# The first quarter of a projection's depth taken in two halves, its modulation loaded by halves, and the first squares summed on TensorE

## The chip, the cores and the metric

The kernel runs on one core of a Trainium2 chip. The metric is the device time of one execution in microseconds; the time before is the median of three executions. Engines are named as in the profile: PE (TensorE) multiplies, DVE (VectorE), ACT (ScalarE) and POOL (GpSimd) work on elements, SP (SyncE) issues the transfers.

## The reference

One step of a two-layer transformer for 128 context tokens and 128 latent tokens. All that matters here is the first sub-layer of layer 0:

```
mod = silu(cond) @ w_ada[l] + b_ada[l]
sh1, sc1, gt1, sh2, sc2, gt2 = jnp.split(mod[:, None, :], 6, axis=-1)
h = rmsnorm(x, g_norm_mix[l]) * (1 + sc1) + sh1
proj = h @ w_in
```

`x` has 2048 features. `mod` is a product of two condition rows (context and latent) with a 2048 x 12288 matrix, and `proj` has 23 blocks of 128 columns. Everything is fp32. After it come the two attentions, the output projection, a convolutional FFN and a second layer of the same size; the change leaves these alone.

## The kernel before, in words

The features lie on the partitions: the residual stream `x` is 16 chunks of 128 features by 256 tokens. A weight product is made of two fp32r parts: a raw tile of weights is split into `wh` (ACT, L212) and `wl = raw - wh` (DVE, L213), and each block of 128 x 128 weights takes three PE products, `wh*hx_high`, `wh*hx_low` and `wl*hx_high` (L305, L306, L309 in `gemm` and `first_three`'s L291 to L293). A raw tile is 1 MB, 16 blocks; three buffers `raw` hold such tiles, four buffers `wh` and four `wl` hold half a tile each, three PSUM banks `acc` take the sums.

The first projection (`mixer_ab`, L732 to L753) goes over its depth in four quarters q of four chunks each. In each quarter the four chunks of `x` are modulated into `hx` (`modulate`, L476 to L509: DVE multiplies by the spread norm, DVE and ACT apply scale and shift, ACT casts the high part, DVE or POOL subtracts the low part), then 23 column blocks c are multiplied: 12 PE products each. ACT copies the sum of q=0 into `pr` or `qb` (L745); DVE adds those of q=1 to 3 to it (L747).

The modulation comes in **units** (l, j, q): 512 columns of part j (0 is the shift, 1 the scale) of layer l, 4 MB in four tiles of 1 MB. Unit order is the list `ROWS`: (0,1,0), (0,0,0), (0,1,1), (0,0,1) and so on, so units 0 and 1 serve quarter q=0, units 2 and 3 serve q=1, units 4 and 5 serve q=2. A tile is loaded into one of two buffers `araw` (L421) and multiplied by the condition in four PE instructions into the bank `ada` (L401, `sum_rows`); it is freed by this product. After the fourth tile, ACT copies the bank (L342), PE transposes it (L349), DVE reduces it and adds the bias (L358, L360), and for j=1 makes the scale (L367). `pump` calls `row_step` a number of times for each column block (`RATE["in"]` rows; a quarter of a tile a call), and `ensure` finishes the units that a quarter needs. In the start phase (`ada["both"]`) every second tile takes a `raw` buffer instead.

The norm of the stream (L1029 to L1034) squares the 16 chunks on ACT (L165, L168), adds them up on POOL (L172), sums over the partitions with four PE products (L192, L193); then `rstd` adds eps on DVE (L177) and takes the power on POOL (L179), `diagonal` scales the identity on DVE (L199) and `spread` multiplies it by ones on PE (L207).

The order on each engine is not the order of the text: a scheduler places the instructions of the program by its own estimate of times, within what the buffers allow, except those wrapped in `tc.keep_in_program_order`. Each engine, and SP's list of transfers, then keeps the built order: an instruction that waits holds up all behind it on its engine. The order of the built programs of both kernels is known before a run.

Of the kernel before, what the change touches and what calls it, by code (L numbers as in the profile page):

```python
# [17 lines left out]
P = 128  # L18
D = 2048
KD = D // P  # L20
T = 128
# [62 lines left out]
def step_kernel(ctx: ExitStack, tc: tile.TileContext, A: dict):  # L84
# [52 lines left out]
    def load_cw(l):  # L137
        ada["cw"] = T_(keep, [P, 4, 2 * NFF], "convw")
        sp.dma_start(out=ada["cw"], in_=A["wconv"][:, l])

# [32 lines left out]

    def rstd(ps, n):

        v = T_(small, [P, 2], "rv")
        dve.tensor_scalar(out=v[:, :n], in0=ps, scalar1=EPS, scalar2=None, op0=ALU.add)  # L177
# [10 lines left out]
    def stat_rstd(st, width, bank=bank):  # L188
        ps = bank()
        for g in range(2):  # L190
            t = slice(g * T, (g + 1) * T)
            pe.matmul(ps[:, g:g + 1], st["acc"][:, t], inv(width), start=True, stop=False)  # L192
            pe.matmul(ps[:, g:g + 1], st["last"][:, t], inv(width), start=False, stop=True)  # L193
        return rstd(ps[:, 0:2], 2)

# [117 lines left out]

    ada = {"i": 0, "t": 0, "due": 0.0, "pew": 1.0, "both": True}
    feat = {"i": 0, "t": 0, "due": 0.0}
    stage = ["ab"]
    pinned = [False]
    done = set()
    later = []

    def vector(name, l, j, q):
# [84 lines left out]
    def row_step(until=len(ROWS)):  # L406
# [9 lines left out]
        if g == 0:  # L416
            if ada["both"] and t % 2:
                ada["raw"] = T_(wpool, [P, 4, 512], "raw")
            else:
                ada["raw"] = T_(wpool, [P, 4, 512], "araw", bufs=2)  # L420
            sp.dma_start(out=ada["raw"], in_=A["w_ada"][l, j, q, t])  # L421
# [200 lines left out]
    def mixer_ab(hx, rb0, st):  # L622
        l = 0
        with tc.tile_pool(name="ab", bufs=1) as ab:
            with tc.tile_pool(name="abp", bufs=1) as pj:
# [7 lines left out]
                def caches():  # L633
                    sp.dma_start(out=ckc, in_=A["cache_ckv"])
                    split(kv_in[:, :, 0, T:2 * T], kv_in[:, :, 1, T:2 * T], ckc)
                    sp.dma_start(out=kr[:, T:2 * T], in_=A["cache_krope"])
                    sp.dma_start(out=kg[:, :, T:2 * T], in_=A["cache_gqa_k"])
                    sp.dma_start(out=vg[:, 1], in_=A["cache_gqa_v"])

# [49 lines left out]
                def keys(c):  # L689
# [7 lines left out]
                    r = rstd(pst[:, 0:2], 2)  # L697
                    yield
# [32 lines left out]

                W = Weights(A["w_in_ab"], 4, 4, cycle=23)  # L732
                for q in range(4):
                    ensure(0, 1, [q])
                    ensure(0, 0, [q])
                    ada["both"] = False
# [4 lines left out]
                    for c in range(23):  # L741
                        ps = gemm(W.chunk(), lambda k: hx[:, 4 * q + k, :NT], lambda k: hx[:, 4 * q + k, NT:2 * NT])
                        to = pr[:, c] if c < 15 else qb[:, c - 15]
                        if q == 0:
                            act.copy(to, ps)  # L745
                        else:
                            dve.tensor_tensor(out=to, in0=to, in1=ps, op=ALU.add)  # L747
                        if q == 3:
                            finish(c)
                        if q < 3:  # L750
                            pump(RATE["in"], until=2 * (q + 2))
                        else:
                            pump(RATE["in3"])  # L753

            with tc.tile_pool(name="abh", bufs=1) as hp:
# [10 lines left out]
                def gqa_query(h):  # L766
# [8 lines left out]
                    r = rstd(pst[:, 0:2], 2)  # L775
                    pool.tensor_scalar(out=rsb[:, h], in0=r[:, 0:2], scalar1=HEAD_SCALE,
# [322 lines left out]
def _layout(i):  # L1099
# [29 lines left out]

    a["w_ada"] = i["w_ada"].reshape(NL, 4, 4, P, 6, 4, 512).transpose(0, 4, 5, 1, 3, 2, 6).copy()  # L1130
    for l, j, q in FEATS:
        w = i["w_ada"][l][:, j * D + 512 * q:j * D + 512 * q + 512]
        a["w_ada"][l, j, q] = w.T.reshape(4, P, 4, 512)
# [4 lines left out]
    w = np.concatenate([w, np.zeros((D, P), np.float32)], 1)  # L1138
    a["w_in_ab"] = np.concatenate([_blocks(w[512 * q:512 * q + 512], range(24), 4) for q in range(4)])
    w = i["w_mla_q_up"][0].reshape(768, 8, 192)  # L1140
# [47 lines left out]
```

## Time and profile before

| | |
|---|---|
| median of three executions | 2388.5 us (2387.7 to 2389.89) |
| the profiled execution | 2393.79 us, its span 2391.9 us |
| PE busy | 2329.2 us, 97% of the span |
| first projection product | 40.30 us after the span's start |
| first product of q=1, of q=2, of q=3 | 85.89, 135.66, 179.04 us |

In the rows of the profile, a timeline row gives the start, the time, the engine, the line, the operation with what it writes and reads, and in brackets how long the engine had been idle and what ended this. Several like instructions in a row are merged (x4). The tile product of L401 is four instructions, counted as x8. A row of stretches gives for each engine its busy time and count, then the clock that TensorE was granted, the busy share of the transfer engines and GB/s. Lines with `L401` are the modulation products, `L305`, `L306` and `L309` the projection products.

### The profile page before, as it was taken

The page shows a single profiled execution, that of the slowest core. Times are in us where ns is not written, and L with a number is a line of the kernel's source. Part 1 is how long each engine was busy: PE and PEld are TensorE (multiplying, and loading weights), DVE is VectorE, ACT ScalarE, POOL GpSimd, SP SyncE. Part 2 cuts the span into 40 slices and gives each one's busy share as a digit, 9 for nine tenths or more (in the row PEclk, how much of TensorE's full clock was granted, in tenths as well). Part 3 has the DMA queues.
Part 4 walks back from the last instruction along what each step waited for, and adds up shares of the span by engine and source line. Part 5 has one row for each costly group of instructions (what it writes and reads, how often), then busy time and mean ns, then how long its engine had stood idle before and what let it go on. Part 6 is the DMA issues. An engine that isn't in the chain of part 4 may idle for free. (4 is left out here: it accounts for less than half of the span.)

```text
span 2391.9 us, 47275 instructions
## 1 busy us (share of the span) xinstructions
PE 2329.2 (97%) x19664; PEld 2189.5 (92%) x19664; DVE 1764.9 (74%) x2691; ACT 1165.7 (49%) x1815; POOL 180.2 (8%) x219
## 2 busy tenths in 40 slices
PE   6999999999999999999999999999999999999997
PEld 3778868789999999999989999997999999999997
DVE  2467534469999999999979777877899855666654
ACT  4335544365554345554465444445655534555542
POOL 2002101110000000001220000023000000000011
PEclk9999999999999999999999999999999999999998
DMA  9886678877777777777766787686667655555553
GB/s 382 310 338 239 235 265 306 311 274 256 263 262 282 289 276 263 264 264 264 303 229 237 279 296 293 257 301 260 249 250 261 214 194 194 194 194 194 194 194 120
DMA packets 92549, 612.92 MB, mean 256 GB/s; under 512 B 9968, under 2 KB 17840, under 8 KB 20400
## 3 DMA queue, kind: packets, MB, share of 16 engines
q1 hardware_dynamic: 92336, 609.91, 69.6%
q8 instruction: 154, 2.52, 0.4%
q14 instruction: 59, 0.48, 0.1%
HBM read 605.12 MB, written 4.75 MB: 255 GB/s over the span
## 5 line engine op out<-in xcount | busy, mean ns | idle before, releaser
L212 ACT CAST wh<-raw 128x1024 fp32r<-128x1024 f32 (+1 forms) x788 | 795.5, 1015 | 984.0 <-PE acc L306 823.6
L213 DVE TENSOR_TENSOR wl<-raw,wh 128x1024 fp32r<-128x1024 f32 (+1 forms) x788 | 921.6, 1183 | 390.7 <-ACT wh L212 384.7
L305 PE MATMUL acc<-hx,wh 128*128 128x256 f32 x4064 | 1132.9, 279 | 8.6 <-ACT hx L504 5.6
L309 PE MATMUL acc<-hx,wl 128*128 128x256 f32 x4064 | 1131.0, 279 | 0.0
L306 PE MATMUL acc<-hx,wh 128*128 128x256 f32 x4064 | 1130.2, 278 | 0.0
L305 PEld LDWEIGHTS acc<-hx,wh 128*128 128x128 f32 x4064 | 765.9, 189 | 34.8 <-issue 12.1
L306 PEld LDWEIGHTS acc<-hx,wh 128*128 128x128 f32 x4064 | 766.5, 189 | 13.8 <-issue 12.9
L309 PEld LDWEIGHTS acc<-hx,wl 128*128 128x128 f32 x4064 | 766.2, 189 | 12.2 <-issue 10.4
L306 PE MATMUL acc<-g,wh 128*128 128x256 f32 x1408 | 388.3, 276 | 0.0
L309 PE MATMUL acc<-g,wl 128*128 128x256 f32 x1408 | 388.0, 276 | 0.0
L305 PE MATMUL acc<-g,wh 128*128 128x256 f32 x1408 | 387.8, 276 | 0.0
L386 DVE CUSTOM_DVE_ANT_0 junk<-araw,condb 128x2048 f32<-128x2048 f32 x120 | 275.0, 2291 | 0.0
L306 PEld LDWEIGHTS acc<-g,wh 128*128 128x128 f32 x1408 | 264.3, 188 | 0.0
L309 PEld LDWEIGHTS acc<-g,wl 128*128 128x128 f32 x1408 | 264.2, 188 | 0.0
L305 PEld LDWEIGHTS acc<-g,wh 128*128 128x128 f32 x1408 | 264.1, 188 | 0.0
L172 POOL TENSOR_TENSOR sqacc<-sqacc,sq 128x256 f32<-128x256 f32 x76 | 93.0, 1223 | 1534.1 <-issue 1223.1
L401 PE MATMUL ada<-araw,condw 128*32 128x512 f32 x768 | 106.6, 628 | 19.3 <-DMA araw<-w_ada 18.5
L430 DVE SCALAR_TENSOR_TENSOR aacc<-araw,condw,aacc 128x512 f32<-128x512 f32 x150 | 111.8, 773 | 0.2
L553 DVE SCALAR_TENSOR_TENSOR x<-acc,mod,x 128x128 f32<-128x128 f32 x192 | 58.3, 345 | 56.5 <-PE acc L309 55.5
L974 ACT ACTIVATE cv<-acc,convw 128x256 f32<-128x256 f32 x176 | 98.5, 560 | 1.4 <-PE acc L293 1.4
L980 DVE SCALAR_TENSOR_TENSOR cv<-acc,convw,cv 128x254 f32<-128x254 f32 x176 | 84.4, 480 | 3.5
L977 DVE SCALAR_TENSOR_TENSOR cv<-acc,convw,cv 128x254 f32<-128x254 f32 x176 | 83.8, 476 | 2.6 <-ACT cv L974 2.5
(221 smaller groups left out, 1840.1 us busy)
## 6 DMA issues: line engine op xcount, KB each, us to landing
araw<-w_ada SPq DMA_DIRECT2D x188, 1024.0 KB, 5.8
raw<-w_up SPq DMA_DIRECT2D x176, 1024.0 KB, 4.8
raw<-w_down SPq DMA_DIRECT2D x88, 1024.0 KB, 4.8
raw<-w_in_c SPq DMA_DIRECT2D x48, 1024.0 KB, 5.0
raw<-w_in_ab SPq DMA_DIRECT2D x20, 1024.0 KB, 7.0
raw<-w_out_ab SPq DMA_DIRECT2D x16, 1024.0 KB, 6.8
raw<-w_out_c SPq DMA_DIRECT2D x16, 1024.0 KB, 5.2
raw<-w_q_up SPq DMA_DIRECT2D x6, 768.0 KB, 4.7
```

The source lines that it names most:

```text
L172: pool.tensor_tensor(out=st["acc"], in0=st["acc"], in1=sq, op=ALU.add)
L212: pin(act.copy(out_hi, src))
L213: pin(dve.tensor_tensor(out=out_lo, in0=src, in1=out_hi.bitcast(F32), op=ALU.subtract))
L305: fixed(pe.matmul(ps[:, :n], wh, xh(k), start=(i == 0), stop=False))
L306: fixed(pe.matmul(ps[:, :n], wh, xl(k), start=False, stop=False))
L309: fixed(pe.matmul(ps[:, :n], wl, xh(k), start=False, stop=(i == last)))
L386: tc.keep_in_program_order(dve.tensor_tensor_reduce(out=T_(feat["pool"], [P, D], "junk"), in1=feat["row"][:, c], in0=feat["raw"].rearrange ...
L401: i = pe.matmul(ada["ps"][32 * g:32 * g + 32, :], condw[:, 4 * t + g, :], raw[:, g], start=(t == 0), stop=(t == 3), skip_group_check=True)
L430: i = dve.scalar_tensor_tensor(out=acc[:, c], in0=raw[:, g], scalar=condw[:, k, c:c + 1], in1=acc[:, c], op0=ALU.mult, op1=ALU.add)
L974: pin(act.activation(y, ps, AF.Identity, scale=cw[:, 1, m:m + 1], bias=cw[:, 3, m:m + 1]))
L977: pin(dve.scalar_tensor_tensor(out=y3[:, :, 1:], in0=p3[:, :, :T - 1], scalar=cw[:, 0, m:m + 1], in1=y3[:, :, 1:], op0=ALU.mult, op1=ALU.add))
L980: pin(dve.scalar_tensor_tensor(out=y3[:, :, :T - 1], in0=p3[:, :, 1:], scalar=cw[:, 2, m:m + 1], in1=y3[:, :, :T - 1], op0=ALU.mult, op1=A ...
```

## The change

Its parts, as the text and the built order have them:

- `x` is loaded before anything but the constants. Its squares are no longer added on POOL: each of the 16 squared chunks goes to PE as the weights of two products with one column (L1083 after), one for each group of tokens, summed in two banks. `rstd` adds eps in two instructions then.
- Units 0 and 1 are loaded by halves, two columns of chunks each: `load_half` loads two tiles of 1 MB (8 depth blocks of 256 columns), `half_unit` multiplies them in 16 PE instructions of 256 columns, copies, transposes twice and reduces. The first halves of both units are loaded right after `x` (into `araw` and `raw`), the second halves during the first half of the projection.
- The quarter q=0 of the projection becomes two halves of two chunks: 23 column blocks of 6 products each, twice, with the weights laid out to match (8 column blocks of 2 depth blocks a tile). The first half is copied by ACT, the second added by DVE, so 23 evictions are added.
- Units 2 and 3 are pumped in the second half only, at twice the rate.
- The four cache loads and the convolution's weights keep the program's order: SP has the caches inside q=2 (before, between the first modulation tiles), and the convolution's weights in the heads' stage (before, behind the caches).

In the built order of the changed kernel, PE has the two tiles of unit 0's second half ahead of the first projection product; DVE has the two `wl` subtractions of the first projection tile ahead of the additions in `rstd`; the first three tiles of unit 2 stand among the second half's column blocks (before its first, behind its third, behind its tenth) and the fourth behind its sixteenth; all four tiles of unit 3 stand behind the last column block, then the transposes, then two tiles of unit 4, then q=1. SP has the loads of unit 3's third and fourth tile with a projection tile between them. From unit 4's third tile on, both programs have the tiles at nearly the same column blocks.

```diff
-        dve.tensor_scalar(out=v[:, :n], in0=ps, scalar1=EPS, scalar2=None, op0=ALU.add)
+        at = 0
+        for ps in cols:
+            w = n // len(cols)
+            dve.tensor_scalar(out=v[:, at:at + w], in0=ps, scalar1=EPS, scalar2=None, op0=ALU.add)
+            at += w
...
+    def load_half(j, h, tag):
+        raws = [T_(wpool, [P, 4, 512], tag, **({"bufs": 2} if tag == "araw" else {})) for _ in range(2)]
+        for t, raw in enumerate(raws):
+            sp.dma_start(out=raw, in_=A["w_ada"][0, j, 0, 2 * h + t])
+        return [raw.rearrange("p g n -> p (g n)").rearrange("p (b n) -> p b n", b=8) for raw in raws]
+
+    def half_unit(j, h, raws):
+        ps = T_(ppool["ada"], [P, 512], "ada", bufs=1)
+        for k in range(KD):
+            g = k % 4
+            pe.matmul(ps[32 * g:32 * g + 32, :NT], condw[:, k, :], raws[k // 8][:, k % 8],
+                      start=(k < 4), stop=(k >= KD - 4), skip_group_check=True)
+        am = T_(tmp, [P, 512], "am", bufs=1)
+        act.copy(am[:, :NT], ps[:, :NT])
+        pt = T_(ppool["ada"], [P, 512], "ada", bufs=1)
+        for b in range(2):
+            pe.transpose(pt[:, b * P:(b + 1) * P], am[:, b * P:(b + 1) * P], ident)
...
+                def part(W, k0, n, first, rate, between=None, **kw):
+                    for c in range(23):
+                        ps = gemm(W.chunk(), lambda k: hx[:, k0 + k, :NT], lambda k: hx[:, k0 + k, NT:2 * NT])
+                        to = pr[:, c] if c < 15 else qb[:, c - 15]
+                        if first:
+                            act.copy(to, ps)
+                        else:
+                            dve.tensor_tensor(out=to, in0=to, in1=ps, op=ALU.add)
+                        if between:
+                            between(c)
+                        pump(rate, **kw)
+                def second_half(c):
+                    if c == 3:
+                        second[1] = load_half(1, 1, "araw")
+                    elif c == 9:
+                        half_unit(1, 1, second[1])
+                        second[0] = load_half(0, 1, "araw")
+                    elif c == 17:
+                        half_unit(0, 1, second[0])
+                for h in range(2):
+                    modulate(hx, rb0, 0, 0, range(2 * h, 2 * h + 2))
+                    W = Weights(A["w_in_ab"][3 * h:3 * h + 3], 2, 8, cycle=23)
+                    if h == 0:
+                        part(W, 0, 2, True, 0, second_half)
+                    else:
+                        part(W, 2, 2, False, 2 * RATE["in"], until=4)
...
-        for i in range(8):
-            row_step()
         for c in range(0, KD, 4):
             sp.dma_start(out=x[:, c:c + 4], in_=A["xT"][:, c:c + 4])
-        st = stat_init()
+        first = {1: load_half(1, 0, "araw"), 0: load_half(0, 0, "raw")}
+        ps = [bank(), att_bank()]
         for c in range(KD):
-            stat_add(st, x[:, c], KD)
+            sq = T_(tmp, [P, NT], "sq", bufs=2)
+            act.activation(sq, x[:, c], AF.Square)
+            for g in range(2):
+                pe.matmul(ps[g][:, 0:1], sq[:, g * T:(g + 1) * T], inv(D), start=(c == 0), stop=(c == KD - 1))
+        rb0 = spread(diagonal(rstd([p[:, 0:1] for p in ps], 2), (0, 1)))
+        for j in (1, 0):
+            half_unit(j, 0, first[j])
         hx = T_(keep, [P, KD, ROW], "hx", F32R)
-        rb0 = norm_scale(st)
```

More of the change, by code (lines that the diff above doesn't have):

```diff
@@ L138, in load_cw @@
         ada["cw"] = T_(keep, [P, 4, 2 * NFF], "convw")
-        sp.dma_start(out=ada["cw"], in_=A["wconv"][:, l])
+        tc.keep_in_program_order(sp.dma_start(out=ada["cw"], in_=A["wconv"][:, l]))
     chains = []
@@ L310, in gemm @@
         return ps[:, :n]
-    ada = {"i": 0, "t": 0, "due": 0.0, "pew": 1.0, "both": True}
+    ada = {"i": 2, "t": 0, "due": 0.0, "pew": 1.0}
     feat = {"i": 0, "t": 0, "due": 0.0}
@@ L319, in step_kernel @@
     later = []
+    def load_half(j, h, tag):
[14 more added lines that the diff above has]
+            pe.transpose(pt[:, b * P:(b + 1) * P], am[:, b * P:(b + 1) * P], ident)
+        at = slice(2 * h, 2 * h + 2)
+        out = mod[:, 0, j, at]
+        dve.tensor_reduce(out=out, in_=pt[:, :NT].rearrange("p (b g r) -> p b r g", b=2, g=4)[:, :, 0:2],
+                          axis=AX.X, op=ALU.add)
+        dve.tensor_tensor(out=out, in0=out, in1=vector("bada", 0, j, 0)[:, at], op=ALU.add)
+        if j == 1:
+            dve.scalar_tensor_tensor(out=scl[:, 0, 0, at], in0=out, scalar=1.0,
+                                     in1=vector("gmix", 0, 0, 0)[:, at], op0=ALU.add, op1=ALU.mult)
+        if h == 1:
+            done.add((0, j, 0))
     def vector(name, l, j, q):
@@ L416, in row_step @@
         if g == 0:
[L417 to L420, printed above, removed]
+            ada["raw"] = T_(wpool, [P, 4, 512], "araw", bufs=2)
             sp.dma_start(out=ada["raw"], in_=A["w_ada"][l, j, q, t])
@@ L730, in finish @@
                         start(values(1))
-                W = Weights(A["w_in_ab"], 4, 4, cycle=23)
-                for q in range(4):
+                def part(W, k0, n, first, rate, between=None, **kw):
[9 more added lines that the diff above has]
+                        pump(rate, **kw)
+                second = {}
+                def second_half(c):
[13 more added lines that the diff above has]
+                        part(W, 2, 2, False, 2 * RATE["in"], until=4)
+                W = Weights(A["w_in_ab"][6:], 4, 4, cycle=23)
+                for q in range(1, 4):
                     ensure(0, 1, [q])
                     ensure(0, 0, [q])
-                    ada["both"] = False
                     pinned[0] = q == 3
@@ L740, in mixer_ab @@
                     modulate(hx, rb0, 0, 0, range(4 * q, 4 * q + 4))
[L741 to L753, printed above, removed]
+                    if q < 3:
+                        part(W, 4 * q, 4, False, RATE["in"], until=2 * (q + 2))
+                    else:
+                        part(W, 4 * q, 4, False, RATE["in3"], finish)
             with tc.tile_pool(name="abh", bufs=1) as hp:
@@ L1130, in _layout @@
     a["w_ada"] = i["w_ada"].reshape(NL, 4, 4, P, 6, 4, 512).transpose(0, 4, 5, 1, 3, 2, 6).copy()
+    for j in (1, 0):
+        w = i["w_ada"][0][:, j * D:j * D + 512].reshape(2, 8, P, 2, 256)
+        a["w_ada"][0, j, 0] = w.transpose(3, 0, 2, 1, 4).reshape(4, P, 4, 512)
     for l, j, q in FEATS:
```

19 lines of the change are left out of this document (10 added, 9 removed).

## The prediction

> **What bounds the kernel now.** I read the page's totals and its row of slices first, then the busy time of each engine by stretch, then the order of events in the first 140 us.
>
> ```profile
> span 2391.9 us, 47275 instructions
> PE 2329.2 (97%) x19664; PEld 2189.5 (92%) x19664; DVE 1764.9 (74%) x2691; ACT 1165.7 (49%) x1815; POOL 180.2 (8%) x219
> PE   6999999999999999999999999999999999999997
> ...
> core 0: us, PE busy (x) PEld busy (x) DVE busy (x) ACT busy (x) POOL busy (x), PEclk, DMA share, GB/s
> 0.00:40.30 40.30, 19.46 (x91) 5.41 (x91) 6.89 (x20) 13.46 (x29) 11.98 (x20) 0.96 0.98 393
> 40.30:80.10 39.80, 39.80 (x320) 34.89 (x320) 17.04 (x22) 21.41 (x39) 1.62 (x2) 0.95 0.89 348
> 85.90:131.90 46.00, 46.00 (x348) 36.33 (x348) 23.90 (x43) 13.18 (x16) 1.62 (x2) 0.93 0.82 303
> ...
> 25.00:30.00 5.00, 3.91 (x18) 1.58 (x22) 3.11 (x11) 0.00 (x0) 1.10 (x1) 1.00 1.01 419
> ```
>
> TensorE is busy 97% of the span; only the first slice (60 us) falls to 6 tenths. Until 40.30 the transfers are the bound (share 0.98, 393 GB/s), from then on TensorE. So the change can only win in the first 40 us, and only what is not given back before the quarters q=1 to 3 run as they do now.
>
> ```profile
> 6.19 0.23 ACT L135 ACTIVATE condw<-cst 128x32 f32<-128x32 f32 x1
> ...
> 22.43 0.33 SPq L421 DMA_DIRECT2D araw<-w_ada  x1
> 24.86 1.09 PE L349 MATMUL ada<-cst,am 128*128 128x128 f32 x4
> 25.03 0.16 DVE L177 TENSOR_SCALAR rv<-misc 128x2 f32<-128x2 f32 x1 [25.03 <-PE misc L193]
> 27.04 1.19 PE L207 MATMUL misc<-diag,cst 128*128 128x256 f32 x2 [1.09 <-DVE mod L358]
> 28.16 1.94 PE L401 MATMUL ada<-araw,condw 128*32 128x512 f32 x8
> 28.27 1.42 DVE L494 TENSOR_TENSOR nt<-x,misc 128x256 f32<-128x256 f32 x4 [0.88 <-PE misc L207]
> 29.87 1.40 PE L401 MATMUL ada<-raw,condw 128*32 128x512 f32 x8
> 34.51 1.99 ACT L212 CAST wh<-raw 128x1024 fp32r<-128x1024 f32 x2 [10.78 <-DMA raw<-w_in_ab]
> 35.58 2.36 DVE L213 TENSOR_TENSOR wl<-raw,wh 128x1024 fp32r<-128x1024 f32 x2 [5.90 <-ACT wh L212]
> 38.30 1.66 ACT L503 ACTIVATE nt<-nt,mod,scl 128x128 f32<-128x128 f32 x4 [1.31 <-DVE mod L360]
> 40.30 1.01 PE L305 MATMUL acc<-hx,wh 128*128 128x256 f32 x3 [0.25 <-ACT hx L504]
> ```
>
> Today two whole units (8 MB) and the first projection tile, landed at 34.51, must be there before the first projection product at 40.30.
>
> **Part 1, the start.** In the new order SP loads the constants (0.72 MB), the stream (2.10 MB), four half-unit tiles and the first projection tile: 8.06 MB. Today the constants, the stream and five tiles are those same bytes, and the issue at 22.43 is the one that waits for the fifth tile. So the projection tile lands at about 22.5 instead of 34.51. From here the built order decides: VectorE has both wl subtractions of this tile ahead of the additions that open the rstd. By the rows 34.51 and 35.58 + 2.36 a tile takes 3.43 us to be split: 25.9. From the rv addition to the first nt multiplication the rows give 28.27 - 25.03 = 3.24, plus 0.16 for the second addition: the scale is spread at 29.3. Then TensorE has both tiles of the next half unit ahead of the projection. I take 1.94 for the first and 1.40 for the second, since the rows 28.16 and 29.87 are this pair in this place, right behind a spread. **First projection product: 29.3 + 1.94 + 1.40 = 32.6**, where 40.30 stands now. A half-unit tile has twice the instructions on half the columns; I take it as equal. The modulation of two chunks starts at 29.3 too and takes under 3.2 us (nt 0.7 for two; then 2.0 from 38.30 to 40.30 for four chunks), so it hides behind those tiles; without them 32.0 would stand here.
>
> The sum of squares leaves POOL for 32 one-column products on TensorE, in pairs:
>
> ```profile
> 23.58 0.57 PE L193 MATMUL misc<-cst,sq 128*128 128x1 f32 x2
> 24.00 0.56 PE L192 MATMUL misc<-cst,sqacc 128*128 128x1 f32 x2
> ...
> 195.40 0.36 PE L192 MATMUL misc<-cst,sqacc 128*128 128x1 f32 x2
> 195.62 0.36 PE L193 MATMUL misc<-cst,sq 128*128 128x1 f32 x2
> ...
> 41.10 0.41 PE L306 MATMUL acc<-hx,wh 128*128 128x256 f32 x1
> 41.32 0.41 PE L309 MATMUL acc<-hx,wl 128*128 128x256 f32 x1
> ...
> 44.29 0.28 PE L306 MATMUL acc<-hx,wh 128*128 128x256 f32 x1
> ...
> 61.80 0.28 PE L306 MATMUL acc<-hx,wh 128*128 128x256 f32 x1
> 61.91 0.28 PE L309 MATMUL acc<-hx,wl 128*128 128x256 f32 x1
> 62.11 1.06 PE L401 MATMUL ada<-araw,condw 128*32 128x512 f32 x8
> 63.11 0.39 PE L305 MATMUL acc<-hx,wh 128*128 128x256 f32 x1
> ```
>
> One such product costs 0.42 at the start and 0.22 later; projection products are 0.22 apart at 41.10 and 0.11 at 61.80, a tile's product 1.94 or 1.06. ScalarE is free for the first square at 6.4, so the first pair stands at about 6.9. All at the slow pace, 16 pairs (13.4), three half-unit tiles and five eighths of a fourth (7.0) and two transposes (0.5) end at 27.8, 1.9 behind the 25.9 above; at the fast pace after some 4 us they end near 21 and are hidden. I take hidden and keep +1.9 for the range. [...]
>
> POOL's 14 additions are gone; nothing else waits for POOL there.
>
> **Part 2, the two halves.** The stretch from 40.30 to 80.10 is today's q=0: 276 products, 5 tiles, one set of transposes in 39.8 us. In the change the same 276 products start at the fast pace (18 products at 0.21 instead of 0.11 fall away, -1.8), and carry 6 tiles (+1.1) and two more pairs of transposes (+0.6): 39.7, so the 276th ends at **72.3**.
>
> ```profile
> L747 DVE TENSOR_TENSOR proj<-proj,acc x45: 412/420/424, 92.9 to 206.9; 128x256 f32<-128x256 f32 x45
> 50.48 0.37 ACT L745 COPY proj<-acc 128x256 f32<-128x256 f32 x1
> ```
>
> The 23 further evictions (0.42 each on VectorE, 9.7 us) lie in a stretch where VectorE has 17.04 of 39.8 us; ScalarE's 23 copies of 0.37 and six casts of 1.0 now fall into some 19 us. With three accumulators and 0.68 us per chunk, a cast ahead of a copy (1.37) just fits into two chunks. I take 0; if it doesn't fit, 0.3 at each of 11 casts, +3.
>
> **Part 3, the way into q=1.** Here the gain goes. A modulation load needs one of two buffers, freed by TensorE's product of the load before last. In the built order the four tiles of unit 3 all stand behind the 276th product. The third is issued only when the first is multiplied, the fourth when the second is; and between them SP has a projection tile. Then two tiles of unit 4 stand ahead of the first q=1 product, the second of them issued only after unit 3's last.
>
> ```profile
> 80.14 1.92 PE L401 MATMUL ada<-araw,condw 128*32 128x512 f32 x16
> 82.77 0.66 PE L349 MATMUL ada<-cst,am 128*128 128x128 f32 x4 [0.71 <-ACT am L342]
> 85.89 1.01 PE L305 MATMUL acc<-hx,wh 128*128 128x256 f32 x3 [2.47 <-ACT hx L504]
> 88.75 1.94 PE L401 MATMUL ada<-araw,condw 128*32 128x512 f32 x8
> ...
> DMA to landing us min/median/max: 4.8/6.4/9.2
> ...
> araw<-w_ada SPq DMA_DIRECT2D x14, 1024.0 KB, 6.9
> ```
>
> Today two tiles stand there, both landed, and 3.8 us pass from their end (82.06) to q=1 (85.89). In the change: first tile done 73.4; third issued, alone in the queue, landed after the least time, 4.8: 78.2; the projection tile and the fourth behind it at 2.5 each (1.05 MB at the 419 GB/s of the stretch from 25 to 30): 83.2; its product at the slow pace after the idle time, 1.94: 85.1; 3.8 to the modulated chunks: 88.9. But unit 4's second tile, issued at 85.1, lands at 89.9, and its product takes 1.06 to 1.94: **q=1 starts at 91.4**. Today's q=1 starts at 85.89 and does those two tiles inside (2.0 at the slow pace, 1.1): 88.95 at equal work. That is +2.45. Of today's slow start (20 products at 0.21, 2.0 us) I give the change half back, since TensorE is in work from 85.5 but for about 1 us: **+1.45**.
>
> **Part 4, what is moved.** The four cache loads (0.59 MB, 1.5 us of the queue) go from the start, where they were in the way, into SP's list inside q=2, and the convolution weights (0.18 MB) into the heads. From unit 4's third tile on, tiles and products stand as today to within a few places, so I take 0; if a modulation load behind the caches was just in time, +1.5.
>
> **The sum.** -7.7 at the first product, -1.8 for the pace, +1.7 for tiles and transposes, and the rest is given back in the 19 us from 72.3 to 91.4, where today 5.8 pass: +1.45, say **+1.5 us**. The profiled execution took 2393.79 against a median of 2388.5; I set the change on the median: **2390.0 us**.
>
> **The rivals.**
> - *Loaded landings, slower.* The three loads in a row of part 3 take not the least 4.8 but the 6.9 that is the median of later modulation loads: 3 x 2.1 = +6.3, in all +7.8, 2396.3. Against it: the queue should be nearly empty by then. It decides from about 1.1 us more on each.
> - *The gain stands, faster.* Up to unit 3's last tile 30.9 MB must land; at today's 393 GB/s that is 78.5 instead of 83.2. If loads run ahead so that only bytes count and unit 4's second tile is in time, q=1 starts at 78.5 + 1.1 + 3.8 = 83.4, 8.0 earlier: -6.5, 2382.0. For it: the queue ran at that rate for 40 us. Against it: the built order ties the loads to products.
> - *Squares stay slow.* +1.9 in part 1, 2391.9: still within 0.2%.
>
> **How the numbers follow.** 0.2% (4.8 us) is about what a measurement of this kernel can tell from no change. Within it: 0.56, my forecast with the slow squares (0.12 of it). Slower: 0.26, the loaded landings 0.18, and 0.08 for ScalarE's casts (+3), the caches (+1.5) and the slow squares (+1.9) coming together. Faster: 0.18, the gain that stands. The forecast with one open term at a time reaches from 2389 to 2393; the range takes in both rivals, to leave out no more than 2 in 10: 2381 to 2397.
>
> **What would show it.** Right: the first projection product at 32 to 33 us at a pace of 0.11; the 276th at 72 to 73; then TensorE idle for two waits on modulation loads of 3 to 5 us; q=1 near 91. Wrong: rv much later than 26 (squares slow); waits on proj copies inside the first half (ScalarE); no wait of TensorE behind the 276th product, or q=1 before 86 (the gain stands); landings near 7 us there (loaded).

## The result, and the profile after

| | before | changed |
|---|---|---|
| median of the runs side by side (six each) | 2389.57 us (2387.7 to 2392.36) | 2398.7 us (2396.68 to 2402.84) |
| ratio to before, 95% interval | | 1.0038 (1.0025 to 1.0051) |
| the profiled execution | 2393.79 us, span 2391.9 us | 2399.88 us, span 2397.7 us |
| first projection product | 40.30 us | 32.50 us |
| first product of q=1, q=2, q=3 | 85.89, 135.66, 179.04 us | 95.13, 141.68, 185.97 us |

The changed kernel is slower by 0.38%; the forecast was no change, the range ended at 2397. By the profiles it lost 6.1 us, by the medians 9.1. The 3.0 us between the two is where the profiled executions lie: that of before 4.2 above the median of its six runs, that of the changed kernel 1.2 above.

The order of events in the changed kernel (start, time, engine, line; in brackets the idle time ahead and what ended it). Lines have shifted: L309, L310 and L313 are the projection products, L434 the tile products, L336 the half-unit products, L1083 the square sums.

```profile
12.76 0.56 PE L1083 MATMUL misc<-cst,sq 128*128 128x1 f32 x2
13.19 0.56 PE L1083 MATMUL att<-cst,sq 128*128 128x1 f32 x2
...
27.82 0.16 DVE L180 TENSOR_SCALAR rv<-misc 128x1 f32<-128x1 f32 x1 [0.88 <-PE misc L1083]
...
32.50 0.61 PE L309 MATMUL acc<-hx,wh 128*128 128x256 f32 x3 [0.39 <-ACT hx L534]
...
51.86 0.39 PE L309 MATMUL acc<-hx,wh 128*128 128x256 f32 x1 [0.32 <-ACT qb L768]
...
74.17 1.06 PE L434 MATMUL ada<-araw,condw 128*32 128x512 f32 x8
76.47 1.06 PE L434 MATMUL ada<-araw,condw 128*32 128x512 f32 x8 [1.24 <-DMA araw<-w_ada]
81.42 1.93 PE L434 MATMUL ada<-araw,condw 128*32 128x512 f32 x8 [3.88 <-DMA araw<-w_ada]
86.51 1.93 PE L434 MATMUL ada<-araw,condw 128*32 128x512 f32 x8 [3.16 <-DMA araw<-w_ada]
...
93.27 1.93 PE L434 MATMUL ada<-araw,condw 128*32 128x512 f32 x8 [0.72 <-DMA araw<-w_ada]
...
95.13 1.01 PE L309 MATMUL acc<-hx,wh 128*128 128x256 f32 x3
...
185.97 1.01 PE L309 MATMUL acc<-hx,wh 128*128 128x256 f32 x3 [4.11 <-ACT hx L534]
```

The first projection product comes 7.8 us earlier, as forecast. The 276th, the last of q=0, ends just ahead of 74.17, 6 us earlier than before (80.10). Then 21 us pass until q=1, where before 5.8 passed. Two of the six tiles there are unit 4's, which before did inside q=1 (3.1 us, forecast): at equal work -6.1 + (21.0 - 5.8 - 3.1) = +6.0. Between these two profiled executions that is all of the loss; q=2 stands at +6.0 too, q=3 at +6.9, the end at +5.8.

In SP's list of the changed kernel a row is the issue of a load; merged rows give the stretch from the first issue to the last:

```profile
69.99 0.39 SPq L261 DMA_DIRECT2D raw<-w_in_ab  x1
75.29 0.33 SPq L451 DMA_DIRECT2D araw<-w_ada  x1
76.49 0.33 SPq L261 DMA_DIRECT2D raw<-w_in_ab  x1
77.60 11.23 SPq L451 DMA_DIRECT2D araw<-w_ada  x3
```

Unit 3's third tile is issued at 75.29, when the first is multiplied, and is there at 81.42, 6.1 us later; the fourth, behind a projection tile, goes out at 77.60 and is there at 86.51, 8.9 us later. In this time (the view by stretches: busy time of PE, PEld, DVE, ACT, POOL, then the granted clock, the transfers' share and GB/s) TensorE is busy for 1.29 and 1.93 of 5 us each, and its granted clock falls to 0.85 and 0.50:

```profile
75.00:80.00 5.00, 1.29 (x12) 0.16 (x8) 1.36 (x2) 0.20 (x1) 0.00 (x0) 0.85 0.87 328
80.00:85.00 5.00, 1.93 (x8) 0.20 (x8) 0.00 (x0) 0.00 (x0) 0.00 (x0) 0.50 1.01 395
```

### The profile page after: what moved, and what is told of

The parts are those of the page before. It is cut to its first block, busy times and chain, and to the rows that moved or that the text cites. A ratio compares the mean times of both kernels' runs of the same rounds, so it can differ in the third digit from the quotient of the medians.

```text
span 2397.7 us, 47523 instructions
## 1 busy us (share of the span) xinstructions
PE 2342.2 (98%) x19784; PEld 2204.6 (92%) x19784; DVE 1772.9 (74%) x2720; ACT 1164.8 (49%) x1817; POOL 169.9 (7%) x205
## 5 line engine op out<-in xcount | busy, mean ns | idle before, releaser
L309 PE MATMUL acc<-hx,wh 128*128 128x256 f32 x4064 | 1133.9, 280 | 7.8 <-ACT hx L534 4.5
L313 PE MATMUL acc<-hx,wl 128*128 128x256 f32 x4064 | 1131.1, 279 | 0.0
L310 PE MATMUL acc<-hx,wh 128*128 128x256 f32 x4064 | 1129.8, 278 | 0.0
L309 PEld LDWEIGHTS acc<-hx,wh 128*128 128x128 f32 x4064 | 765.6, 189 | 35.6 <-issue 12.1
L313 PEld LDWEIGHTS acc<-hx,wl 128*128 128x128 f32 x4064 | 765.9, 188 | 13.0 <-issue 11.2
L310 PEld LDWEIGHTS acc<-hx,wh 128*128 128x128 f32 x4064 | 766.1, 189 | 8.6 <-issue 7.9
L310 PE MATMUL acc<-g,wh 128*128 128x256 f32 x1408 | 388.3, 276 | 0.0
L313 PE MATMUL acc<-g,wl 128*128 128x256 f32 x1408 | 388.1, 276 | 0.0
L309 PE MATMUL acc<-g,wh 128*128 128x256 f32 x1408 | 387.9, 276 | 0.0
L310 PEld LDWEIGHTS acc<-g,wh 128*128 128x128 f32 x1408 | 264.3, 188 | 0.0
L313 PEld LDWEIGHTS acc<-g,wl 128*128 128x128 f32 x1408 | 264.1, 188 | 0.0
L309 PEld LDWEIGHTS acc<-g,wh 128*128 128x128 f32 x1408 | 264.1, 188 | 0.0
L172 POOL TENSOR_TENSOR sqacc<-sqacc,sq 128x256 f32<-128x256 f32 x62 | 84.7, 1365 | 1521.7 <-issue 1217.7
L434 PE MATMUL ada<-araw,condw 128*32 128x512 f32 x736 | 101.5, 629 | 13.7 <-DMA araw<-w_ada 12.4
```

The costliest lines, as they stand in the source:

```text
L172: pool.tensor_tensor(out=st["acc"], in0=st["acc"], in1=sq, op=ALU.add)
L309: fixed(pe.matmul(ps[:, :n], wh, xh(k), start=(i == 0), stop=False))
L310: fixed(pe.matmul(ps[:, :n], wh, xl(k), start=False, stop=False))
L313: fixed(pe.matmul(ps[:, :n], wl, xh(k), start=False, stop=(i == last)))
L434: i = pe.matmul(ada["ps"][32 * g:32 * g + 32, :], condw[:, 4 * t + g, :], raw[:, g], start=(t == 0), stop=(t == 3), skip_group_check=True)
```

## The experiments

The theory (A): the gain of 6 us at the 276th product is lost behind it, because two buffers tie each load of unit 3 to the product of the load before last, and all four products stand behind the 276th. The rivals: the queue's bytes are the bound (B), or ACT, DVE and the squares in the new start (C). A ratio is that to the kernel before, run alongside: 23 runs with a median of 2391.07 us beside e1 to e4, 35 with 2390.78 beside e5 to e8, 14 with 2390.40 beside e9 to e12.

**e1, a third buffer.**

```diff
-            ada["raw"] = T_(wpool, [P, 4, 512], "araw", bufs=2)
+            n = 4 * ada["i"] + t - 8
+            if ada["i"] < 4 and n % 3 == 2:
+                ada["raw"] = T_(ada["pj"], [P, 4, 512], "third")
+            else:
+                ada["raw"] = T_(wpool, [P, 4, 512], "araw", bufs=2)
...
```

> The changed kernel with a third 1 MB buffer for the tiles of units 2 and 3 (every third tile goes there; the latent cache takes its place in q=3). In the built order unit 2's third tile is then loaded early, unit 3's first two tiles stand among the second half's column blocks, only the last two stay behind the 276th product, both loads are issued ahead of the projection tile that was between them, and unit 4's two tiles move behind the first 36 products of q=1. Theory A (two buffers tie each load to the product of the load before last, so the gain is lost in a chain of waits): no wait of more than 2 us is left behind the 276th product, q=1 starts near 84 instead of 95.1, and since unit 4's two tiles (3.1) are then done inside q=1, the whole is about 8 us faster than the changed kernel, 2388 to 2392. Rival B (the queue is full and only bytes count): unit 3's last tile has two projection tiles (2.1 MB, 5.4 us at 390 GB/s) less ahead of it, q=1 starts near 87 and the whole is about 5 us faster than the changed kernel, 2393 to 2395. Rival C (the time is lost by ACT and DVE in the halves): q=1 moves, the whole stays at 2398.

2389.68 us, ratio 0.9998 (0.9989 to 1.0006): 9.0 us less than the changed kernel, in the range that theory A gave and below that of rival B. The buffer also lets tiles move ahead in the built order, so this run shows the two together. The order of events, and the stretch of the projection's first quarter:

```profile
34.27 0.62 PE L309 MATMUL acc<-hx,wh 128*128 128x256 f32 x3 [0.63 <-ACT hx L538]
...
79.47 1.06 PE L434 MATMUL ada<-araw,condw 128*32 128x512 f32 x8
80.85 1.07 PE L434 MATMUL ada<-araw,condw 128*32 128x512 f32 x8 [0.31 <-DMA araw<-w_ada]
...
85.79 1.01 PE L309 MATMUL acc<-hx,wh 128*128 128x256 f32 x3 [2.46 <-ACT hx L538]
```

```profile
34.27:79.47 45.20, 44.23 (x380) 35.60 (x380) 26.89 (x50) 22.83 (x45) 1.72 (x2) 1.00 0.91 350
```

The waits of 3.9 and 3.2 us are gone, one of 0.31 is left, and q=1 is 9.3 us earlier. But it starts no earlier than before (85.89), though the projection started 6 us earlier and TensorE was in work for 44.23 of 45.20 us. So mending the way into q=1 returns what was lost, and no gain over the kernel before shows (0.9989 to 1.0006); why, e11 and e12 ask.

**e2, projection tiles held back.** Two buffers as in the changed kernel; unit 3's loads and the later projection tiles of q=1 keep the text's order.

```diff
-            sp.dma_start(out=ada["raw"], in_=A["w_ada"][l, j, q, t])
+            i = sp.dma_start(out=ada["raw"], in_=A["w_ada"][l, j, q, t])
+            if ada["i"] == 3:
+                tc.keep_in_program_order(i)
...
+                if self.late is not None and self.at >= self.late:
+                    tc.keep_in_program_order(i)
...
+                    W.late = 3 if q == 1 else None
```

> The changed kernel, two buffers as they are, but SP's loads of unit 3 and the q=1 projection tiles from the fourth on are kept in the text's order: the fourth and fifth projection tile of q=1 are no longer ahead of, or between, unit 3's third and fourth tile. TensorE's order up to q=1 stays. If the landings of 6.1 and 8.9 us of these two tiles come from the projection tiles in the queue (loaded landings), they fall to about 4.8 to 5.5 and q=1 starts near 91.2 instead of 95.1. If they are as long in an empty queue, q=1 stays at 95. Inside q=1 the held projection tiles can be late and give the gain back, so the start of q=1 is what is read, not the whole time (2394 to 2402).

The issue of unit 3's last two loads in SP's list, and the order of events:

```profile
75.55 1.19 SPq L454 DMA_DIRECT2D araw<-w_ada  x2
```

```profile
74.42 1.92 PE L437 MATMUL ada<-araw,condw 128*32 128x512 f32 x16
80.55 1.93 PE L437 MATMUL ada<-araw,condw 128*32 128x512 f32 x8 [4.20 <-DMA araw<-w_ada]
83.00 1.93 PE L437 MATMUL ada<-araw,condw 128*32 128x512 f32 x8 [0.52 <-DMA araw<-w_ada]
...
91.75 1.01 PE L312 MATMUL acc<-hx,wh 128*128 128x256 f32 x3
```

The third tile, issued at 75.55, lands after 5.0 us, the fourth 2.5 us behind it, and q=1 starts at 91.75, 3.4 us earlier. That is the share of the loaded queue; the wait for the third tile stays, for it is that of the chain. The whole is 2404.15 us, ratio 1.0059 (1.0045 to 1.0073), 2 us above what was expected: behind the projection tile of 62.73 SP issues none up to 90, where the changed kernel issues two (69.99, 76.49), and q=3, at 189.33, stands 3.4 us later than there.

**e3, the squares on GpSimd again.**

```diff
...
-            for g in range(2):
-                pe.matmul(ps[g][:, 0:1], sq[:, g * T:(g + 1) * T], inv(D), start=(c == 0), stop=(c == KD - 1))
...
+            stat_add(st, x[:, c], KD)
...
```

> The changed kernel with the first squares added up on GpSimd as before (two halves, loads by halves and the stream first stay). TensorE is free for the half-unit tiles, the norm is known some 5 us earlier (rv near 22 instead of 27.8) and only one half-unit tile stands ahead of the first projection product: it starts near 28 to 29 instead of 32.5. Theory A (what is won ahead of the 276th product is lost in the waits on unit 3's and unit 4's tiles): those waits are bound by loads, q=1 starts within 1.5 us of 95.1 and the whole within 2 us of the changed kernel. Rival C (the squares on TensorE at the slow pace cost the end): about 4 us faster than the changed kernel, 2394 to 2395.

```profile
28.83 1.01 PE L309 MATMUL acc<-hx,wh 128*128 128x256 f32 x3
...
94.85 1.01 PE L309 MATMUL acc<-hx,wh 128*128 128x256 f32 x3
```

Another 3.7 us at the first product, 0.3 at q=1: 2396.53 us, ratio 1.0031 (1.0019 to 1.0043). The squares aren't the loss, and this head start doesn't pass the entry into q=1.

**e4, the stream first and the squares on TensorE, without halves.** The kernel before with

```diff
+        for c in range(0, KD, 4):
+            sp.dma_start(out=x[:, c:c + 4], in_=A["xT"][:, c:c + 4])
         for i in range(8):
             row_step()
...
```

and the squares of the change.

> The kernel before with the stream loaded first and its squares summed on TensorE, and nothing else: no halves, units 0 and 1 loaded whole, caches and convolution weights as before. Here the first projection product waits for units 0 and 1 (8 MB) and the first projection tile, not for the norm. If the squares and the order of the stream cost nothing by themselves (theory A): within 2 us of the kernel before, 2388 to 2392, the squares' pairs again 0.86 apart up to about 24 us. If they carry the loss (rival C): slower by 3 us or more.

```profile
41.79 0.62 PE L309 MATMUL acc<-hx,wh 128*128 128x256 f32 x3 [1.11 <-ACT hx L508]
...
85.78 0.62 PE L309 MATMUL acc<-hx,wh 128*128 128x256 f32 x3 [2.46 <-ACT hx L508]
```

2389.4 us, ratio 0.9991 (0.9982 to 1.0000). These two parts by themselves cost nothing that the runs could show. The first product comes 1.5 us later than before, at the fast pace (0.62 for three), and q=1 stands where it stood: the kernel before had lost about as much by its first 18 products at the slow pace (0.21 apart instead of 0.11).

**e5, the third buffer and the squares on GpSimd.** The edits of e1 and e3.

> The third buffer of e1 and the squares on GpSimd of e3 together. e1 started the projection at 34.3 and had q=1 at 85.8, its last unit-3 tile waiting 0.3 us for its load; e3 started at about 28. Theory B (with the third buffer the queue's bytes are the bound): q=1 starts at 84 to 86, TensorE waits for unit 3's last loads again, and the whole is within 2 us of e1 (ratio to before 0.999 to 1.0005). Rival (TensorE's work is the bound): the whole start moves, q=1 near 80.5 and the whole 5 us faster than e1 (ratio 0.9975).

```profile
29.35 1.01 PE L309 MATMUL acc<-hx,wh 128*128 128x256 f32 x3 [3.03 <-ACT hx L538]
...
55.98 0.62 PE L309 MATMUL acc<-hx,wh 128*128 128x256 f32 x3 [2.36 <-ACT hx L538]
...
85.38 0.62 PE L309 MATMUL acc<-hx,wh 128*128 128x256 f32 x3 [2.46 <-ACT hx L538]
```

2389.81 us, ratio 0.9998 (0.9988 to 1.0008), as e1: 4.9 us at the first product are 0.4 at q=1. The miss is in the place: unit 3's last tile waits for no load; the time goes earlier, at the slow pace of the first products (1.01 for three, 0.62 in e1) and in 2.36 us ahead of the second half.

**e6 and e7, odd tiles in the weight buffers** (e7 with the squares on GpSimd).

```diff
-            ada["raw"] = T_(wpool, [P, 4, 512], "araw", bufs=2)
+            if ada["i"] in (2, 3) and t % 2:
+                ada["raw"] = T_(wpool, [P, 4, 512], "raw")
+            else:
+                ada["raw"] = T_(wpool, [P, 4, 512], "araw", bufs=2)
```

> The changed kernel, but every second tile of units 2 and 3 is loaded into one of the three weight buffers raw (as every second tile of the first units was before), so units 2 and 3 have two plus up to three buffers and the projection tiles of q=1 can't run ahead of them. In the built order all eight tiles and both sets of transposes stand ahead of the second half's last products, and unit 4's first two tiles too. Theory A (the entry into q=1 is lost to tiles behind the last product): no idle time behind the last product of the second half but at most 1 us; q=1 starts near 81 with unit 4's two tiles already done, 8 us ahead of the kernel before at equal work (85.9 + 3.1 = 89): ratio 0.9965 to 0.998. Rival B (bytes): the second half's last weights now come behind the modulation tiles, TensorE waits for wh or wl inside the second half for 3 us or more, ratio 0.998 to 1.0005.

> e6 with the first squares on GpSimd: the first projection product moves from about 32.5 to about 28.5. If TensorE's work is the bound in e6, another 3 us come out (ratio to before about 0.0013 lower than e6's). If bytes are, the whole is within 1.5 us of e6.

In e6 all of units 2 and 3 is done when unit 4's first tile stands at 76.79, and then TensorE waits for weights:

```profile
76.79 1.06 PE L434 MATMUL ada<-araw,condw 128*32 128x512 f32 x8 [0.28 <-DVE mod L391]
80.22 0.58 PE L309 MATMUL acc<-hx,wh 128*128 128x256 f32 x1 [2.37 <-ACT wh L216]
```

e6: 2390.87 us, ratio 0.9998 (0.9989 to 1.0008); e7: 2388.23 us, 0.9988 (0.9979 to 0.9998). Rival B holds here, with a wait of 2.4 us where it named 3 or more: with the modulation in time, the projection's weights are late, and q=1 starts at 89.24, level with the kernel before at equal work (89) and not at the 81 of theory A. e7 is 0.0010 below e6, between its two expectations. Of the kernels that load all their tiles it is the only one whose interval lies below 1: by 2.6 us, and one interval of ten that ends at 0.9998 can be chance.

**e8, the kernel before with the cache and convolution loads moved.**

```diff
-                    sp.dma_start(out=ckc, in_=A["cache_ckv"])
+                    tc.keep_in_program_order(sp.dma_start(out=ckc, in_=A["cache_ckv"]))
```

and likewise the other four loads.

> The kernel before with only the program order kept for the four cache loads and the convolution weights: 0.77 MB leave the queue ahead of the first projection product and stand inside q=2 and the heads. The first projection product comes 1.9 us earlier (38.4 instead of 40.3). Theory A (what is won at the start is lost in the way into q=1, as long as unit 3's tiles stand behind the last product; here too the last of them is among the last): 0 to -2 us. Rival (the loads moved into q=2 delay the modulation tiles there, and the cache's split is late at q=3): q=3's first product waits more than today's 2.87 us, 1.5 us or more slower.

The order of events in e8, then the row of the kernel before for the first product of q=3:

```profile
38.15 0.62 PE L305 MATMUL acc<-hx,wh 128*128 128x256 f32 x3 [1.73 <-ACT hx L504]
...
84.63 1.01 PE L305 MATMUL acc<-hx,wh 128*128 128x256 f32 x3 [2.46 <-ACT hx L504]
...
172.88 0.60 PE L349 MATMUL ada<-cst,am 128*128 128x128 f32 x4
...
177.58 1.01 PE L305 MATMUL acc<-hx,wh 128*128 128x256 f32 x3 [4.11 <-ACT hx L504]
```

```profile
179.04 0.62 PE L305 MATMUL acc<-hx,wh 128*128 128x256 f32 x3 [2.87 <-ACT hx L504]
```

2390.25 us, ratio 0.9994 (0.9985 to 1.0002). -2.15 us at the first product, -1.26 at q=1, and the wait ahead of q=3 grows from 2.87 to 4.11 us, +1.24, as in the changed kernel (its row 185.97). No load is late there: in this build the transposes of q=3's last unit (172.88) are the last thing ahead of q=3, while before products still ran beside them. The other profiles go with the moved loads: the wait is 4.11 in e1, e3, e5 to e7 and e9 to e11, which move them, 2.87 in e4 and 3.02 in e12, which don't; only e2 has another order there. Which of the five loads does it wasn't tried. On the whole e8 still reaches q=3 1.46 us ahead of the kernel before.

**e9, the changed kernel again.**

> The changed kernel once more, unaltered. Its first profile was 6.1 us longer than the profile of before, its median 9.1. If the entry into q=1 is what varies (three landings in a row, each as long as the queue happens to be loaded), the ratio comes out at 1.0025 to 1.004 again and the profile shows the waits of 1.2, 3.9 and 3.2 us behind the last product in other sizes, all else before 72 us equal to 0.5. If the 3 us lie elsewhere, the entry is the same and a later stage is longer.

```profile
27.85 0.57 PE L1083 MATMUL att<-cst,sq 128*128 128x1 f32 x2
...
33.70 0.62 PE L309 MATMUL acc<-hx,wh 128*128 128x256 f32 x3
...
87.20 1.94 PE L434 MATMUL ada<-araw,condw 128*32 128x512 f32 x8 [3.33 <-DMA araw<-w_ada]
...
94.96 0.62 PE L309 MATMUL acc<-hx,wh 128*128 128x256 f32 x3
...
182.98 1.01 PE L309 MATMUL acc<-hx,wh 128*128 128x256 f32 x3 [4.11 <-ACT hx L534]
```

2397.85 us, ratio 1.0032 (1.0021 to 1.0044). The waits behind the 276th product are the same to 0.5 us (0.75, 3.95, 3.33), and so is q=1 (94.96). Two other things differ. The last squares are at the slow pace here (0.57 for two at 27.85, 0.36 at 27.64 in the first profile), and the first product comes at 33.70, 1.2 us later than in the first profile; q=1 takes that in. And q=1's first products are fast here (0.62 for three), slow in the first profile (1.01, until about 99 us): q=3 stands at 182.98, 3.0 us earlier. Neither expectation had these places.

**e11 and e12, 4.2 MB less to load**, in the changed kernel and in the one before.

```diff
-        if g == 0:
+        if g == 0 and not (ada["i"] in (2, 3) and t % 2):
```

> The changed kernel with 4.2 MB less to load: every second tile of units 2 and 3 isn't loaded, TensorE multiplies the tile before it again, so the modulation of q=1 is left out in part; all engine work is the same. In the built order units 2 and 3 then end inside the second half, with three tiles of unit 4 behind them. If the bytes of the queue are what takes the gain (theory B), it stands now: q=1 starts near 82 with three unit-4 tiles done, where the kernel before would stand at 90 with the same work: ratio 0.9955 to 0.997. If it isn't bytes, but the work of TensorE or of ACT and DVE in the halves, the ratio stays above 1.000.

> The kernel before with the same 4.2 MB left out in the same way: the control of e11. Its start (40 us) is bound by units 0 and 1 as before; the waits of 3.2 us at the entry into q=1 go, and part of the later waits on modulation loads: ratio 0.998 to 0.9988. The difference of e11 and e12, about 0.0020 (5 us) in e11's favour, is what the two halves are worth when bytes don't bind; if e11 isn't faster than e12, the halves win nothing even then.

e11 (L309), then e12 (L305):

```profile
33.80 0.62 PE L309 MATMUL acc<-hx,wh 128*128 128x256 f32 x3
...
126.10 0.62 PE L309 MATMUL acc<-hx,wh 128*128 128x256 f32 x3 [0.53 <-ACT hx L534]
...
171.07 1.01 PE L309 MATMUL acc<-hx,wh 128*128 128x256 f32 x3 [4.11 <-ACT hx L534]
```

```profile
38.10 3.32 PE L401 MATMUL ada<-araw,condw 128*32 128x512 f32 x16 [0.41 <-DVE mod L358]
41.35 0.86 PE L305 MATMUL acc<-hx,wh 128*128 128x256 f32 x3
...
128.73 0.62 PE L305 MATMUL acc<-hx,wh 128*128 128x256 f32 x3
...
172.55 1.01 PE L305 MATMUL acc<-hx,wh 128*128 128x256 f32 x3 [3.02 <-ACT hx L504]
```

e11: 2383.24 us, ratio 0.9971 (0.9960 to 0.9983); e12: 2384.48 us, 0.9973 (0.9962 to 0.9984). The changed kernel is then 15 us faster than with all loads, where theory B has it; but the kernel before gains 6 us by the same, where 3 to 5 were expected, and the two are equal within their intervals: 1.2 us apart where 5 were expected. So the halves win next to nothing even where no load of units 2 and 3 binds. The 7.55 us of head start (33.80 against 41.35) are 2.6 at q=2 and 1.5 at q=3. Of the 4.9 that are gone by q=2, 4.3 are no loss but work that changed places: before its first projection product e12 multiplies ten tiles (units 0 and 1, and the two of row 38.10), e11 six, by q=2 both have multiplied 26, and four tiles are 4.3 us at 1.06 to 1.07. The last 1.1 is the wait ahead of q=3 (4.11 against 3.02).

**e10, wide products beside the squares.**

```diff
+        wide = att_bank()
...
+            pe.matmul(wide[:, :NT], ones, sq, start=(c == 0), stop=(c == KD - 1))
```

> The changed kernel with one further product of 256 columns (ones by the squared chunk, into a bank that nobody reads) behind each pair of one-column products. In the changed kernel TensorE was in work from 6.8 to 27.4 us, but the pairs stayed 0.86 apart. If one-column products leave the pace slow because they hold hardly any columns, the wide ones end the slow pace within about 5 us of 7 us: a pair is then 0.45 apart, a half-unit tile of eight 0.53 to 0.6 instead of 0.97. If something else keeps the pace slow until 27 us, the pairs stay 0.86 apart, and the squares end 10 us later. Only the start is read.

```profile
29.33 1.20 PE L1085 MATMUL att<-sq,cst 128*128 128x256 f32 x2
30.46 2.47 PE L336 MATMUL ada<-raw,condw 128*32 128x256 f32 x24
32.86 0.38 PE L1084 MATMUL misc<-cst,sq 128*128 128x1 f32 x2
```

The wide products don't end the slow pace: squares and single tiles keep it (0.57 for two narrow products at 12.20, 0.56 at 28.90, 1.94 for a half-unit tile at 15.46) until a run of one and a half tiles (row 30.46; a half-unit tile counts as x16, this row as x24), and are fast behind it (0.38 and 0.36 for two narrow products at 32.86 and 33.11). So a wide product beside each pair isn't enough; that the narrow ones still hold the pace back isn't excluded, since the wide ones fill 1.0 of each 1.7 us. The whole is 2400.38 us (three runs), ratio 1.0045 (1.0030 to 1.0060). The first projection product stands at 48.89 here, 16.4 us later than in the changed kernel, and q=1 at 97.81, only 2.7 later: of the waits on unit 3's and unit 4's loads 0.46 us is left. The entry into q=1 takes in a late start as it takes in the early one of e3.

## Why the prediction was wrong

The mechanism of part 3 was the right one: TensorE waits behind the 276th product, on the loads that were named, by 3.9 and 3.2 us where 3 to 5 were forecast. The terms of the sum were mis-sized, nearly all to one side, and the squares of part 1 weren't hidden.

| step | forecast | measured |
|---|---|---|
| first projection product | 32.6 | 32.50 |
| end of the 276th product | 72.3 | 74.1 |
| unit 3's third tile, issue and landing | 73.4 + 4.8 | 75.29 + 6.1 |
| its fourth tile, behind the third | 5.0 | 5.1 |
| from there to q=1 | 8.2 | 8.6 |
| first product of q=1 | 91.4 | 95.13 |
| credit for q=1's slow start | -1.0 | 0 |

The entry into q=1 is 3.7 us later than forecast, and the credit fell away: 1.45 + 3.7 + 1.0 = +6.15, and q=2 starts 6.0 us later than before, the profiled executions differ by 6.09. (At q=3 the distance is 6.9, at the end 5.8.) So the sum closes for this pair of executions, and the terms that failed are these:

- **The third landing (1.3 us).** It was taken from the least of the profile, 4.8, as of a load alone in the queue; it took 6.1, since a projection tile issued at 69.99 was still under way (the two issued at 69.99 and 76.49 took 7.4 and 8.9 us to land). e2 takes the projection tiles away: 5.0. This is the rival of the loaded landings, with a fifth of its price. Against that rival stood "the queue should be nearly empty by then"; the stretch 75 to 80 has a share of 0.87, and 80 to 85 one of 1.01.
- **The 276th product (1.8 us, of part 2).** Half a microsecond is TensorE's wait for ACT's copy at the end of the first half (row 51.86; 0.60 from product to product, 0.11 elsewhere): that much of the 23 evictions, taken as 0, shows. The added tile and the two pairs of transposes cost 0.4 more than the lone durations that were added up (a tile among products takes 1.2, not 1.06). The last 0.9 is in no single event; the traces here don't tell where it comes from.
- **The credit (1.0 us).** It was argued from TensorE being in work from 85.5 on. In the first profile q=1 started slow (1.01 for three), as before, in e9 fast (0.62): it is a matter of the execution, and between the two profiles compared above it is 0.
- **The base.** The forecast was set on 2388.5, the median of three runs; beside the changed kernel six runs gave 2389.57, and in later rounds 35 gave 2390.78.

By the medians the loss is larger, 9.1 us and in e9's round 7.5, and this sum doesn't hold the rest. It isn't in e9's profile either: 3.9 us behind the kernel before at q=3, 4.6 at the end. The record shows where to look. Of the 72 executions of the kernel before in the rounds of e1 to e12, 24 had a mean granted clock of 0.994 or more and a median of 2387.7 us, 28 had 0.990 or less and 2391.7; the 12 of the changed kernel (e9's with them) lie at 0.989 to 0.992 with a median of 2398.1. Against the former the loss is 10.4, against the latter 6.4. Like with like this isn't, since the mean of the changed kernel takes in the stretches of its waits, at 0.67 (75 to 85 us) and 0.50 (85 to 95); what sets the executions of the kernel before apart, and so what the other 1 to 3 us are, stays open.

The first product came to 0.1 us where it was forecast, by luck. The squares stayed slow (rv at 27.82, where 25.9 was taken and 27.8 kept for the range, +1.9); from there the scale was spread 0.9 sooner than taken, the two tiles ahead of the projection took 1.94 instead of 3.34, and a wait of 0.39 for hx came on top. In e9 the slow pace lasts longer (0.57 at 27.85), and the first product stands at 33.70. That the squares reach the fast pace after some 4 us was the author's estimate; the projection products did so (0.21 apart from 41.10 on, 0.12 from 44.29), but no run shows it for squares alone: they are still 0.43 apart in the rows 12.76 and 13.19, 6 us after the first of them, and in e10, where wide products stand between them, two of them still take 0.56 at 28.90. Part 4's price of 0 for the moved loads missed an order, not a late load: the wait ahead of q=3 is 1.24 longer (e8), near the 1.5 that were kept for a late load.

The rival "the gain stands" is refuted twice: bytes don't let it (e6 waits 2.4 us for weights instead), and with bytes to spare (e11 against e12) there is hardly a gain to stand (1.5 us at q=3). It counted the earlier first product as time won; four tiles that TensorE did for nothing, while it waited for loads, now stand in its way.

## What to carry to other kernels

An engine that idles at the start is not a gain to be had if it already does later work in that time: count what stands ahead of the first product in both orders, and only then the head start. Where loads rotate through two buffers and their products are all placed behind a stage, the stage's early end turns into waits on landings, one for each tile (here 1.2, 3.9 and 3.2 us); look in the built order for the products that free the buffers. Here a third buffer gave the 9.0 us back, and no more. Price a landing by the queue as it is at that moment (6.1 us here), not by the profile's least (4.8), and let a control with the same bytes taken away from both kernels say what a change is worth.

## What was not expected of the hardware

The slow pace of TensorE did not end with time in work. In the changed kernel it was busy for all of the 20.63 us from 6.77 to 27.40, by squares and single tiles, and the one-column products stayed 0.43 apart (rows 12.76 and 13.19 of the first fence); the pace rose near the end of a run of one and five eighths tiles (row 23.89 below, x26; its products are 0.21 apart up to 26.44), and the squares behind it, at 27.40 and 27.64, are 0.24 apart. In e9 the like run of 3.62 us, from 23.85, wasn't enough: the squares and the tile behind it stayed slow (0.57 at 27.85), and the pace rose within the next two tiles, near 32 (2.20 for x32 from 31.38, against 1.94 in the changed kernel). In e10, with products of 256 columns between, the slow pace lasted beyond 30.46 (2.47 for x24). In e3, which has no squares there, two tiles did it (1.94 at 12.84, then 1.48 at 15.24). The row of the changed kernel, then those of e3:

```profile
23.89 3.58 PE L336 MATMUL ada<-raw,condw 128*32 128x256 f32 x26
```

```profile
15.24 1.48 PE L336 MATMUL ada<-araw,condw 128*32 128x256 f32 x16 [0.46 <-DMA araw<-w_ada]
18.39 0.38 PE L196 MATMUL misc<-cst,sqacc 128*128 128x1 f32 x2 [1.67 <-POOL sqacc L172]
```

No one length of time in work fits these rows: in e3 the two tiles, 3.42 us of work with 0.46 idle between, were enough, in e9 a run of 3.62 us wasn't, and the fp32 squares, alone or with wide products between, with single tiles among them, left the pace slow for 17 us in the changed kernel (6.77 to 23.89) and 18 us in e10 (12.20 to 30.46). What distinguishes tiles from squares is open: no run here has tiles of 128 weight columns, or squares of another type. The granted clock in the view by stretches of the changed kernel reads 1.00 all the while (10 to 30 us), so at the start it is the distance of the rows that tells the pace.
